# Score products on 64 rows in pairs, and a mask added by VectorE, in a one-core hybrid decoder layer

## The chip, the core and the metric

The kernel runs on one core of a Trainium2 chip. The core has TensorE (matrix products, PE in the rows; its weight loads are listed as PEld), VectorE (DVE), ScalarE (ACT), GpSimd (POOL) and SyncE (SP, which issues the DMAs). [...] The metric is the device time of one execution in microseconds; lower is better.

## What is computed

The reference is one decoder layer on 512 positions of width 1024: a token mixer (a gated MLP over chunks and a sparse attention), a cross-attention into 256 memory tokens, and a squared-ReLU MLP. The change touches the sparse attention. With 512 positions, top-16 selection picks all 8 blocks, so the selected branch and the window branch are both plain causal attention, each with keys and values of its own:

```python
s = jnp.einsum('bthgd,bhtmd->bhgtm', qc, kg) * scale
p = masked_softmax(s, mask)          # mask: key_pos <= t
o = g[..., 0:1] * o_cmp + g[..., 1:2] * o_slc + g[..., 2:3] * o_win
```

There are 8 query heads of 64 channels, in 2 groups of 4 that share a key head.

## The kernel before

**Precision.** Numbers that enter a product are split into a high part of type fp32r and a low part that is the rest. A product of two split operands is the sum of high x high, low x high and high x low, three TensorE products into one PSUM tile.

**Scores.** A query tile is 128 positions of one head. `qprep` puts the high and the low part of the query, 64 channels each, into one tile of 128 rows, `qT`. `KB` (its tile is called `b` in the trace) holds the high part of the keys on both halves of the rows, so that one product over 128 rows gives high x high plus low x high. `KL` holds the low part of the keys, on the half of the rows where the query's high part lies, and zeros on the other half, so that a second product over 128 rows gives high x low. A third product, `idb` (the identity) by `tri` (0 or -1e38, bf16), adds the causal mask to the last 128 columns. So a score tile is KB, KL, tri.

**Units and steps.** `units` lists (query tile t, key head, pair of heads): 4 x 2 x 2 = 16 units, and each unit takes two steps. Query tile t sees nb = t+1 key blocks, n = 128 nb columns a branch. For t = 0 and 1 ("early") both branches of a head fit in one bank (2n is 256 or 512 columns); for t = 2 and 3 ("late") each branch of a head has a bank of its own (384 or 512 columns). Before, step e of a unit does head e, both branches. `Pair.scores` makes the products, `Pair.soft` takes the row maximum on VectorE (TENSOR_REDUCE) and the exponential with its row sum on ScalarE, `Pair.scale` multiplies by gate over row sum, `Pair.turn` (one step pair later) transposes the probabilities on TensorE, and `Pair.values` multiplies them with the values.

**Order.** The program is recorded by a class `Plan` and issued in an order that its list scheduler works out: each engine has a fixed order when the program is built. The scheduler takes the costs of `Plan.cost` and a priority of each operation, its place in the program plus a number by stage out of the table `LEADS`. On TensorE, work of other stages (projections, output products) stands between the steps of the attention. The `w,b`, `w,q` and `b,w` products of the rows are such work.

Of the kernel before, what the change touches and what calls it, by code (L numbers as in the profile page):

```python
# [9 lines left out]
F32 = mybir.dt.float32  # L10
# [46 lines left out]
LEADS = {"ch_f0": -1174, "ch_f1": -1572, "ch_f2": -903, "ch_norm1": 1885, "ch_norm2": 867, "ch_norm3": -7928,  # L57
# [21 lines left out]


class Plan:
# [20 lines left out]
    def __init__(self, tc, share):  # L102
        self.tc, self.nc, self.share = tc, tc.nc, share
        self.ops, self.loads, self.lead, self.queue, self.stage, self.stages = [], [], 0.0, None, None, []
        self.home, self.last, self.reads, self.tables = {}, {}, {}, []
        self.tiles, self.uses, self.caps, self.index = [], [], {}, {}
        for e in self.ENGINES:
            setattr(self, e, self._Engine(self, e))
# [31 lines left out]
    def cost(self, eng, op, aps, func):  # L140
        n = max(self.width(a) for a, _ in aps)
        if eng == "tensor":
            if op == "transpose" and all(a.dtype == F32 for a, _ in aps):
                return 109
            return max(25, n / 2.4 + (15 if n > 200 else 7))
# [10 lines left out]
        if eng == "vector":  # L156
            if op == "reciprocal":
                return 68 + 6.3 * n
            fast = op in ("tensor_scalar", "tensor_copy") and not psum
            return 68 + n / (1.92 if fast else 0.96) + 61 * (scalars > (op == "tensor_reduce")) + part  # L160
# [43 lines left out]
    def add(self, ways, args, kw):  # L204
# [48 lines left out]
        func = next((a for a in args if isinstance(a, OP)), None)  # L253
        ways = [(self.ENGINES.index(e), op, self.cost(e, op, aps, func), self.locks(e, op, reads, writes))
                for e, op in ways]
        self.loads.append(self.load(ways[0][1], args[1]) if ways[0][0] == 0 else 0.0)
# [152 lines left out]
def hybrid_block(ctx, tc, x, mem, norm_mix_g, w_in, sg_ln_g, sg_ln_b, sg_w, sg_b, q_norm_g,  # L409
# [163 lines left out]
    load_x(0)  # L573
    dma(grw, norm_mix_g.rearrange("o (k p) -> (o k) p", p=P))
    w_inv = w_in.rearrange("o (k p) n -> p (o k) n", p=P)
# [90 lines left out]
    for h in range(NKV):  # L666
        pool.memset(KL[(1 - h) * HD:(2 - h) * HD, h].bitcast(F32), 0.0)
# [37 lines left out]
    def put_k(b, c):  # L705
# [26 lines left out]
        for h in range(NKV):  # L732
            nc.scalar.copy(KL[h * HD:h * HD + HD, h, b, :], low[h * HD:h * HD + HD, :])
# [35 lines left out]
    tri = cpool.tile([P, P], BF16, name="tri")  # L769
    tri32 = ztile()[:, :P]  # L770
    pool.memset(tri32, 0.0)
    pool.affine_select(out=tri32, in_=tri32, pattern=[[-1, P]], compare_op=OP.is_ge,
# [138 lines left out]
    def qprep(t, kvh):  # L911
# [6 lines left out]
        qs = qs.rearrange("p (g s d) -> p g s d", g=G, s=2)  # L918
        hi, lo = qs[:, :, kvh, :], qs[:, :, 1 - kvh, :]
# [3 lines left out]
        for g in range(G):  # L923
            nc.tensor.transpose(ps[:, g * P:g * P + P].bitcast(F32R), qs[:, g].rearrange("p s d -> p (s d)"), idr)
# [27 lines left out]
    class Pair:  # L952


        def __init__(self, t, kvh, pr, qT):
            self.t, self.kvh, self.pr, self.qT = t, kvh, pr, qT
            self.nb = t + 1
            self.n = self.nb * P
            self.blocks = [(b, j) for b in range(2) for j in range(self.nb)]
            self.S, self.Ps = [None] * 2, [None] * 2  # L960
            self.mx, self.den = [None] * 2, [None] * 2
            self.pts = None

        def scores(self, e):
            kvh, n = self.kvh, self.n
            g = 2 * self.pr + e
            q = self.qT[:, g * P:g * P + P]
            if 2 * n <= 512:
                S = bank()[:, :2 * n].rearrange("p (b n) -> p b n", b=2)
                for i, k in enumerate((KB, KL)):  # L970
                    nc.tensor.matmul(S, q, k[:, kvh, :, :n], start=i == 0, stop=False)
                nc.tensor.matmul(S[:, :, n - P:n], idb, bc(tri[:, None, :], [P, 2, P]), start=False, stop=True)
                self.S[e] = [S]
            else:
                self.S[e] = []
                for b in range(2):
                    S = bank()[:, :n]
                    for i, k in enumerate((KB, KL)):
                        nc.tensor.matmul(S, q, k[:, kvh, b, :n], start=i == 0, stop=False)
                    nc.tensor.matmul(S[:, n - P:n], idb, tri, start=False, stop=True)  # L980
                    self.S[e].append(S)
            self.mx[e], self.den[e] = small(2), small(2)
            self.Ps[e] = []

        def soft(self, e, b):
            Ss, mx = self.S[e], self.mx[e]
            if len(Ss) == 2:
                dve.tensor_reduce(mx[:, b:b + 1], Ss[b], AX.X, OP.max, negate=True)
            elif b == 0:
                dve.tensor_reduce(mx, Ss[0], AX.X, OP.max, negate=True)  # L990
            S = Ss[b] if len(Ss) == 2 else Ss[0][:, b, :]
            self.Ps[e].append(zpool.tile([P, 512], F32, tag="P", bufs=6, name=nm("P"))[:, :self.n])
            act(self.Ps[e][b], S, AF.Exp, bias=mx[:, b:b + 1], accum_out=self.den[e][:, b:b + 1])

        def scale(self, e):
            h = self.kvh * G + 2 * self.pr + e
            c = small(2)
            dve.reciprocal(c, self.den[e])
            for b in range(2):
                nc.either(("vector", "tensor_scalar"), ("gpsimd", "tensor_scalar"))(  # L1000
                    self.Ps[e][b], self.Ps[e][b], c[:, b:b + 1],
                                   gates[:, self.t, 3 * h + 1 + b:3 * h + 2 + b], OP.mult, OP.mult)

        def turn(self, e, q):

            if self.pts is None:
                self.pts = [b8([P, 2, 4, 2 * P], F32R) for _ in range((2 * self.nb + 3) // 4)]
            blk = self.blocks[4 * q:4 * q + 4]
            n = len(blk)
            if not n:  # L1010
                return None
            ps = bank()
            for i, (b, j) in enumerate(blk):
                nc.tensor.transpose(ps[:, i * P:i * P + P], self.Ps[e][b][:, j * P:j * P + P], idf)
            pv = ps[:, :n * P].rearrange("p (j t) -> p j t", j=n)
            pt = self.pts[q]
            return pv, pt[:, 0, :n, e * P:e * P + P], pt[:, 1, :n, e * P:e * P + P]

        def values(self, ptc):
            po = bank()[:, :2 * P]  # L1020
            for i, (b, j) in enumerate(self.blocks):
                if i == len(self.blocks) - 1:
                    for e in range(2):
                        for s in range(2):
                            nc.tensor.matmul(po[:, e * P:e * P + P], Vc[:, self.kvh, 2 * self.pr + e, :], ptc[:, s, :],
                                             start=False, stop=False)
                for s in range(2):
# [408 lines left out]
```

## Time and profile before

| what | value |
|---|---|
| median of 3 runs | 700.16 us (699.53 to 701.16) |
| profiled execution | 699.56 us, its span 697.8 us |
| PE busy | 689.5 us, 99% |
| DVE busy | 415.2 us, 59% |
| ACT busy | 318.2 us, 46% |
| granted TensorE clock | 1.00 all through |

The span runs from the first to the last instruction of the profiled execution; 1.76 us of its time lie around the span. A product's record is longer than the distance to the next one, since products overlap in the pipeline; what a product takes of TensorE's time is the distance between starts.

### The profile page before, as it was taken

How to read it: one execution, taken by the hardware profiler on the slowest of the kernel's cores; microseconds unless marked ns; L12 is line 12 of the kernel's file. 1: busy time of each engine (PE TensorE's matmuls, PEld its weight loads, DVE VectorE, ACT ScalarE, POOL GpSimd, SP SyncE). 2: the span in 40 equal slices, each digit the busy share in tenths (PEclk: the TensorE clock that was granted, in tenths of full speed). 3: DMA queues.
4: the chain of work that ended last, by engine and by line, in shares of the span. 5: the costliest groups of instructions: out<-in, count | busy, mean ns of one | idle time of the engine just before them, and what ended most of it. 6: DMA issues, size and time to landing. Idle time of an engine off the chain costs nothing.

```text
span 697.8 us, 9634 instructions
## 1 busy us (share of the span) xinstructions
PE 689.5 (99%) x3632; PEld 579.0 (83%) x3632; DVE 415.2 (59%) x791; ACT 318.2 (46%) x634; POOL 79.2 (11%) x120
## 2 busy tenths in 40 slices
PE   8999999999999999999999999999999999999997
PEld 7898878888888788888988888888878888888886
DVE  6578898898999997679842432223224444334423
ACT  6544558877788774586532341424133221112210
POOL 1101103232342130133000000000000000000000
PEclk9999999999999999999999999999999999999999
DMA  9624553552223101323243333323223222232203
GB/s 284 167 86 129 156 156 119 182 189 83 62 61 91 62 1 42 111 62 92 66 116 94 88 90 98 113 74 110 91 91 115 97 91 90 97 112 93 91 0 121
DMA packets 63677, 71.03 MB, mean 102 GB/s; under 512 B 3160, under 2 KB 46928, under 8 KB 63632
## 3 DMA queue, kind: packets, MB, share of 16 engines
q1 hardware_dynamic: 63632, 70.42, 32.8%
q8 instruction: 29, 0.48, 0.3%
q14 instruction: 16, 0.13, 0.1%
HBM read 68.32 MB, written 2.10 MB: 101 GB/s over the span
## 4 chain that ended last, share of the span: by engine, by line
PE 92%; DVE 3%; ACT 3%; DMA 1%; issue 0%; SPq 0%; DVEq 0%; ACTq 0%
PE ps L405 92%; DVE b L405 1%; DVE w L405 1%; ACT w L405 1%; ACT b L405 1%; DMA raw<-in_cmp_w_dram 1%; ACT P L405 1%; DMA raw<-in_w_in_dram 1%; DVE s L405 0%; ACT KL L405 0%; DVE pc L405 0%; ACT z L405 0%; DVE P L405 0%; SPq L405 0%; DVE q L405 0%
## 5 line engine op out<-in xcount | busy, mean ns | idle before, releaser
L405 PE MATMUL ps<-w,q 128*128 128x512 f32 x960 | 225.1, 391 | 0.7 <-ACT z L405 0.7
L405 ACT CAST w<-raw 128x1024 fp32r<-128x1024 f32 (+2 forms) x96 | 98.7, 1029 | 249.5 <-PE ps L405 239.9
L405 PEld LDWEIGHTS ps<-w,q 128*128 128x128 f32 x960 | 178.5, 188 | 37.2 <-ACT z L405 1.1
L405 DVE TENSOR_TENSOR w<-raw,w 128x1024 fp32r<-128x1024 f32 (+2 forms) x113 | 133.0, 1178 | 113.0 <-ACT w L405 112.4
L405 PE MATMUL ps<-w,b 128*128 128x512 f32 (+3 forms) x832 | 188.8, 377 | 0.9 <-DVE w L405 0.7
L405 PEld LDWEIGHTS ps<-w,b 128*128 128x128 f32 (+1 forms) x832 | 142.9, 186 | 27.4 <-DVE w L405 2.7
L405 PE MATMUL ps<-b,w 128*128 128x512 f32 x720 | 164.7, 389 | 0.0
L405 PEld LDWEIGHTS ps<-b,w 128*128 128x128 f32 x720 | 134.8, 188 | 27.9
L405 DVE TENSOR_TENSOR b<-ps,b 128x512 fp32r<-128x512 f32 (+2 forms) x88 | 54.6, 636 | 9.4 <-ACT b L405 6.4
L405 PE MATMUL ps<-b,b 128*128 128x256 f32 x344 | 58.7, 293 | 0.0
L405 DVE CAST q<-b 128x512 fp32r<-128x512 f32 x27 | 11.5, 427 | 70.6 <-PE ps L405 70.5
L405 ACT CAST b<-ps 128x512 fp32r<-128x512 f32 (+1 forms) x84 | 44.0, 552 | 17.6 <-PE ps L405 16.9
L405 PEld LDWEIGHTS ps<-b,b 128*128 128x128 f32 x344 | 49.1, 192 | 1.4
L405 POOL TENSOR_SCALAR P<-P,s,gates 128x128 f32<-128x128 f32 (+3 forms) x55 | 35.4, 653 | 90.2 <-DVE s L405 76.9
L405 ACT ACTIVATE P<-ps,s 128x128 f32<-128x128 f32 (+3 forms) x64 | 33.5, 532 | 4.5 <-DVE s L405 4.3
L405 PE MATMUL ps<-idf,P 128*128 128x128 f32 x192 | 34.9, 281 | 0.0
L405 DVE TENSOR_REDUCE s<-ps 128x2 f32<-128x512 f32 (+3 forms) x56 | 32.5, 602 | 0.3 <-PE ps L405 0.2
L405 POOL TENSOR_TENSOR r<-s,negh 128x1 f32<-128x1 f32 (+2 forms) x25 | 20.2, 808 | 93.9 <-DVE s L405 93.8
L405 ACT ACTIVATE z<-ps 128x512 f32<-128x512 f32 (+3 forms) x43 | 23.0, 581 | 11.6 <-PE ps L405 11.5
L405 DVE TENSOR_TENSOR q<-b,q 128x512 fp32r<-128x512 f32 (+1 forms) x36 | 23.7, 657 | 4.6 <-ACT q L405 3.7
L405 PE MATMUL ps<-b,q 128*128 128x256 f32 (+2 forms) x96 | 26.0, 339 | 0.2 <-ACT q L405 0.2
L405 PEld LDWEIGHTS ps<-idf,P 128*128 128x128 f32 x192 | 23.5, 141 | 1.3
(154 smaller groups left out, 549.3 us busy)
## 6 DMA issues: line engine op xcount, KB each, us to landing
raw<-in_w_ff_dram SPq DMA_DIRECT2D x64, 512.0 KB, 4.0
raw<-in_w_in_dram SPq DMA_DIRECT2D x12, 512.0 KB, 4.5
raw<-in_cmp_w_dram SPq DMA_DIRECT2D x8, 512.0 KB, 4.3
raw<-in_w_out_dram SPq DMA_DIRECT2D x8, 512.0 KB, 3.8
raw<-in_w_mkv_dram SPq DMA_DIRECT2D x8, 512.0 KB, 3.8
b<-in_x_dram SPq DMA_DIRECT2D x8, 256.0 KB, 5.1
raw<-in_w_in_dram SPq DMA_DIRECT2D x8, 256.0 KB, 5.6
b<-in_x_dram SPq DMA_DIRECT2D x4, 512.0 KB, 5.7
```

The costliest lines, as they stand in the source:

```text
L405: getattr(getattr(self.nc, eng), op)(*a, **k)
```

## The change

It does four things. The KL products of the two heads of a unit are done on 64 rows each, head 0 on rows 0 to 63 and head 1 on rows 64 to 127, one after the other in the program; for this `qprep` lays out the second head with low and high swapped, and KL holds the low keys on both halves (four more copies on ScalarE, no zeroing on GpSimd). A late step now does one branch of both heads in place of both branches of one head (`part`). Late score tiles get no tri product: VectorE adds the mask, takes the negated sum's minimum and writes the scores to SBUF in one instruction (`tensor_tensor_reduce`, in the rows ISA with a second, small ISA on `s`), and the exponential reads SBUF. Early tiles keep the tri product. The scheduler's cost of the first product of a pair is 4, and `LEADS` has new numbers throughout.

```diff
@@ Plan.cost, Plan.add
+            if self.beside:
+                self.beside = False
+                return 4
...
+        next_to = self.ops and self.ops[-1][0][0][2] == 4
...
@@ LEADS
-LEADS = {"ch_f0": -1174, "ch_f1": -1572, "ch_f2": -903, "ch_norm1": 1885, "ch_norm2": 867, "ch_norm3": -7928,
+LEADS = {"ch_f0": 528, "ch_f1": -1424, "ch_norm0": -3838, "ch_norm1": -9550, "ch_norm3": -11668,
...
@@ put_k
-            nc.scalar.copy(KL[h * HD:h * HD + HD, h, b, :], low[h * HD:h * HD + HD, :])
+            for half in (0, HD):
+                nc.scalar.copy(KL[half:half + HD, h, b, :], low[h * HD:h * HD + HD, :])
@@ Pair.scores
-                for i, k in enumerate((KB, KL)):
-                    nc.tensor.matmul(S, q, k[:, kvh, :, :n], start=i == 0, stop=False)
-                nc.tensor.matmul(S[:, :, n - P:n], idb, bc(tri[:, None, :], [P, 2, P]), start=False, stop=True)
...
+                for e in heads:
+                    nc.tensor.matmul(S[e], q[e], KB[:, kvh, b, :n], start=True, stop=False)
+
+                for e in heads:
+                    r = slice(e * HD, e * HD + HD)
+                    nc.beside = e == 0
+                    nc.tensor.matmul(S[e], q[e][r], KL[r, kvh, b, :n], start=False, stop=not self.both)
+                for e in heads:
+                    if self.both:
+                        nc.tensor.matmul(S[e][:, :, n - P:n], idb, bc(tri[:, None, T - P:], [P, 2, P]),
+                                         start=False, stop=True)
@@ Pair.soft, late tiles
-                dve.tensor_reduce(mx[:, b:b + 1], Ss[b], AX.X, OP.max, negate=True)
...
+                dve.tensor_tensor_reduce(out=pt, in0=S, in1=tri[:, T - self.n:], scale=-1.0, scalar=3e38,
+                                         op0=OP.add, op1=OP.min, accum_out=mx[:, i:i + 1])
+                act(pt, pt, AF.Exp, bias=mx[:, i:i + 1], scale=-1.0, accum_out=self.den[x][:, i:i + 1])
```

The order on TensorE, at the first late unit (t = 2, key head 0). Names in a row are out<-moving,stationary; `ps_452` and `ps_453` are two score tiles, `b_9_89` is KB, `q_449` the query tile. Before:

```order
L405 MATMUL ps_452<-b_9_89,q_449 128x384
L405 MATMUL ps_452<-KL,q_449 128x384
L405 LDWEIGHTS idb
L405 MATMUL ps_452<-tri,idb 128x128
L405 MATMUL ps_453<-b_9_89,q_449 128x384
L405 MATMUL ps_453<-KL,q_449 128x384
L405 LDWEIGHTS idb
L405 MATMUL ps_453<-tri,idb 128x128
```

The same place of the changed kernel, with the row before and behind:

```order
L411 MATMUL ps_766<-w_765,b_640_735 128x512 x2
L411 MATMUL ps_452<-b_9_89,q_449 128x384
L411 MATMUL ps_453<-b_9_89,q_449 128x384
L411 MATMUL ps_452<-KL,q_449 128x384
L411 MATMUL ps_453<-KL,q_449 128x384
L411 MATMUL ps_457<-idf,P_439 128x128 x2
```

The two KL products (64 rows each now) stand next to each other, the tri products are gone, and products over 128 rows stand on both sides.

A later late step on TensorE (t = 2, key head 1; `ps_519` and `ps_520` are the score tiles, `ps_517` a tile of `values`). Before:

```order
L405 MATMUL ps_519<-b_9_89,q_504 128x384
L405 MATMUL ps_519<-KL,q_504 128x384
L405 LDWEIGHTS idb
L405 MATMUL ps_519<-tri,idb 128x128
L405 MATMUL ps_514<-idf,P_487 128x128
L405 MATMUL ps_517<-b_388_482,b_10_91 128x256 x5
L405 MATMUL ps_520<-b_9_89,q_504 128x384
L405 MATMUL ps_520<-KL,q_504 128x384
```

The changed kernel there:

```order
L411 MATMUL ps_519<-b_9_89,q_504 128x384
L411 MATMUL ps_519<-KL,q_504 128x384
L411 MATMUL ps_514<-idf,P_487 128x128
L411 MATMUL ps_517<-b_388_482,b_10_91 128x256 x2
L411 MATMUL ps_517<-b_389_483,b_10_91 128x256 x4
L411 MATMUL ps_517<-pt_476,Vc 128x128
L411 MATMUL ps_514<-idf,P_487 128x128
L411 MATMUL ps_520<-b_9_89,q_504 128x384
L411 MATMUL ps_520<-KL,q_504 128x384
L411 MATMUL ps_517<-pt_476,Vc 128x128 x3
```

Here the two KL products of the pair don't stand together: products over 128 rows lie between them. Of the 24 pairs in the changed order 18 stand together (all 8 early ones, 5 late ones of 384 columns and 5 of 512) and 6 stand apart (3 of 384, 3 of 512). An early pair is followed by its two tri products:

```order
L411 MATMUL ps_280<-b_9_89,q_278 128x256
L411 MATMUL ps_281<-b_9_89,q_278 128x256
L411 MATMUL ps_280<-KL,q_278 128x256
L411 MATMUL ps_281<-KL,q_278 128x256
L411 LDWEIGHTS idb
L411 MATMUL ps_280<-tri,idb 128x256
L411 LDWEIGHTS idb
L411 MATMUL ps_281<-tri,idb 128x256
```

In this piece the tri products have moved from behind each head's KL product to behind both.

## Rows read from the trace of the kernel before

**Rows 1.** The page: span, busy time of TensorE, TensorE in 40 slices, its clock.
```profile
span 697.8 us, 9634 instructions
PE 689.5 (99%) x3632; PEld 579.0 (83%) x3632; DVE 415.2 (59%) x791; ACT 318.2 (46%) x634; POOL 79.2 (11%) x120
...
PE   8999999999999999999999999999999999999997
...
PEclk9999999999999999999999999999999999999999
```

**Rows 2.** Windows: early steps, t = 2, t = 3; busy us (count) of each engine.
```profile
97.00:179.80 82.80, 82.41 (x483) 68.98 (x481) 73.94 (x184) 64.67 (x164) 22.44 (x38) 1.00 0.43 135
179.80:219.00 39.20, 39.20 (x261) 33.24 (x260) 36.19 (x96) 31.94 (x83) 12.06 (x16) 1.00 0.28 86
219.00:258.00 39.00, 38.84 (x259) 31.68 (x258) 36.94 (x88) 30.08 (x75) 11.45 (x15) 1.00 0.11 36
```

**Rows 3.** Groups of TensorE by shape: rows*columns, out, count, busy us, mean ns.
```profile
L405 PE MATMUL ps<-b,w 128*128 128x512 f32 x720 | 164.7, 389 | 0.0
...
L405 PE MATMUL ps<-tri,idb 128*128 128x128 bf16 x32 | 7.4, 230 | 0.0
...
L405 PE MATMUL ps<-q,z 128*64 128x64 f32 x12 | 0.8, 220 | 0.0
```

**Rows 4.** Timeline of TensorE at a late step: start us, length us, what.
```profile
200.87 0.34 PE L405 MATMUL ps<-b,q 128*128 128x384 f32 x1
201.04 0.34 PE L405 MATMUL ps<-KL,q 128*128 128x384 f32 x1
201.22 0.23 PE L405 MATMUL ps<-tri,idb 128*128 128x128 bf16 x1
201.26 0.42 PE L405 MATMUL ps<-b,q 128*128 128x384 f32 x1
201.52 0.34 PE L405 MATMUL ps<-KL,q 128*128 128x384 f32 x1
...
201.76 0.28 PE L405 MATMUL ps<-idf,P 128*128 128x128 f32 x1
201.88 0.27 PE L405 MATMUL ps<-idf,bT 128*128 128x128 f32 x1
```

**Rows 5.** Timeline of TensorE around two 64-row transposes, 108.9 to 111.2 us.
```profile
108.93 0.84 PE L405 MATMUL ps<-w,b 128*128 128x512 f32 x3
109.70 0.25 PE L405 MATMUL ps<-idr,z 64*128 64x64 f32 x1
109.88 0.33 PE L405 MATMUL ps<-idf,wg 128*128 128x128 f32 x1
109.96 0.48 PE L405 MATMUL ps<-w,b 128*128 128x512 f32 x1
110.37 0.24 PE L405 MATMUL ps<-idr,z 64*128 64x64 f32 x1
110.54 0.97 PE L405 MATMUL ps<-w,b 128*128 128x512 f32 x3
```

**Rows 6.** The weight loads of the same stretch.
```profile
109.16 0.19 PEld L405 LDWEIGHTS ps<-w,b 128*128 128x128 f32 x1
109.70 0.14 PEld L405 LDWEIGHTS ps<-idr,z 64*128 64x128 f32 x1 [0.35 <-issue]
...
110.36 0.14 PEld L405 LDWEIGHTS ps<-idr,z 64*128 64x128 f32 x1 [0.24 <-issue]
```

**Rows 7.** Groups of VectorE by shape.
```profile
L405 DVE TENSOR_TENSOR b<-ps,b 128x512 fp32r<-128x512 f32 x64 | 43.0, 685 | 7.2 <-ACT b L405 6.4
...
L405 DVE TENSOR_REDUCE s<-ps 128x1 f32<-128x512 f32 x16 | 10.4, 676 | 0.0
...
L405 DVE TENSOR_SCALAR s<-s 128x1 f32<-128x1 f32 x22 | 3.3, 148 | 2.3 <-ACT j L405 1.3 <-ACT z L405 1.0
```

**Rows 8.** The group of ScalarE that writes KL.
```profile
L405 ACT CAST KL<-ps 64x512 fp32r<-64x512 f32 x4 | 2.3, 583 | 0.0
```

More of the change, by code (lines that the diff above doesn't have):

```diff
@@ L144, in cost @@
                 return 109
+            if self.beside:
+                self.beside = False
+                return 4
             return max(25, n / 2.4 + (15 if n > 200 else 7))
@@ L159, in cost @@
             fast = op in ("tensor_scalar", "tensor_copy") and not psum
+            if op == "tensor_tensor_reduce":
+                part += 60
             return 68 + n / (1.92 if fast else 0.96) + 61 * (scalars > (op == "tensor_reduce")) + part
@@ L253, in add @@
         func = next((a for a in args if isinstance(a, OP)), None)
+        next_to = self.ops and self.ops[-1][0][0][2] == 4
         ways = [(self.ENGINES.index(e), op, self.cost(e, op, aps, func), self.locks(e, op, reads, writes))
                 for e, op in ways]
-        self.loads.append(self.load(ways[0][1], args[1]) if ways[0][0] == 0 else 0.0)
+        self.loads.append(self.load(ways[0][1], args[1]) if ways[0][0] == 0 and not next_to else 0.0)
         self.tables.append(next((self.TABLES[a] for a in args if isinstance(a, AF) and a in self.TABLES), None))
@@ L573, in hybrid_block @@
     load_x(0)
+    nc.stage = "gain0"
     dma(grw, norm_mix_g.rearrange("o (k p) -> (o k) p", p=P))
+    nc.stage = "kv"
     w_inv = w_in.rearrange("o (k p) n -> p (o k) n", p=P)
@@ L665, in hybrid_block @@
     KL = cpool.tile([P, NKV, 2, T], F32R, name="KL")
-    for h in range(NKV):
-        pool.memset(KL[(1 - h) * HD:(2 - h) * HD, h].bitcast(F32), 0.0)
     VB = b8([P, 2 * NKV * TT, P], F32R)
@@ L768, in hybrid_block @@
     dve.tensor_copy(idb, idf)
-    tri = cpool.tile([P, P], BF16, name="tri")
-    tri32 = ztile()[:, :P]
+    tri = cpool.tile([P, T], BF16, name="tri")
+    tri32 = ztile()
     pool.memset(tri32, 0.0)
-    pool.affine_select(out=tri32, in_=tri32, pattern=[[-1, P]], compare_op=OP.is_ge,
+    pool.affine_select(out=tri32[:, T - P:], in_=tri32[:, T - P:], pattern=[[-1, P]], compare_op=OP.is_ge,
                        fill=NEG, base=0, channel_multiplier=1)
@@ L917, in qprep @@
         qs, qT = qpair()
-        qs = qs.rearrange("p (g s d) -> p g s d", g=G, s=2)
-        hi, lo = qs[:, :, kvh, :], qs[:, :, 1 - kvh, :]
+        hi = bass.AP(qs.tensor, qs.offset, [list(qs.ap[0]), [4 * HD, 2], [3 * HD, 2], [1, HD]])
+        lo = bass.AP(qs.tensor, qs.offset + HD, [list(qs.ap[0]), [4 * HD, 2], [HD, 2], [1, HD]])
+        qv = qv.rearrange("p (a e) d -> p a e d", e=2)
         nc.either(("scalar", "copy"), ("vector", "tensor_copy"))(hi, qv)
@@ L923, in qprep @@
         for g in range(G):
-            nc.tensor.transpose(ps[:, g * P:g * P + P].bitcast(F32R), qs[:, g].rearrange("p s d -> p (s d)"), idr)
+            nc.tensor.transpose(ps[:, g * P:g * P + P].bitcast(F32R), qs[:, g * P:g * P + P], idr)
         nc.scalar.copy(qT, ps)
@@ L958, in __init__ @@
             self.n = self.nb * P
+            self.both = 2 * self.n <= 512
             self.blocks = [(b, j) for b in range(2) for j in range(self.nb)]
-            self.S, self.Ps = [None] * 2, [None] * 2
+            self.S, self.Ps = {}, {}
             self.mx, self.den = [None] * 2, [None] * 2
             self.pts = None
-        def scores(self, e):
-            kvh, n = self.kvh, self.n
[L966 to L969, printed above, removed]
-                for i, k in enumerate((KB, KL)):
-                    nc.tensor.matmul(S, q, k[:, kvh, :, :n], start=i == 0, stop=False)
-                nc.tensor.matmul(S[:, :, n - P:n], idb, bc(tri[:, None, :], [P, 2, P]), start=False, stop=True)
-                self.S[e] = [S]
-            else:
[L975 to L983, printed above, removed]
@@ L985, in soft @@
-        def soft(self, e, b):
-            Ss, mx = self.S[e], self.mx[e]
-            if len(Ss) == 2:
-                dve.tensor_reduce(mx[:, b:b + 1], Ss[b], AX.X, OP.max, negate=True)
[L989 to L993, printed above, removed]
@@ L995, in scale, with slot, part, scores @@
-        def scale(self, e):
-            h = self.kvh * G + 2 * self.pr + e
+        def slot(self, b, j):
+            return b * (self.nb if self.both else 4) + j
+        def part(self, x, i):
+            return (x, i) if self.both else (i, x)
+        def scores(self, x):
+            kvh, n = self.kvh, self.n
+            if x == 0 or not self.both:
+                b = slice(0, 2) if self.both else slice(x, x + 1)
+                heads = range(2)
+                q = [self.qT[:, (2 * self.pr + e) * P:(2 * self.pr + e + 1) * P] for e in heads]
+                S = [bank()[:, :n * (b.stop - b.start)].rearrange("p (b n) -> p b n", n=n) for e in heads]
+                for e in heads:
[8 more added lines that the diff above has]
+                                         start=False, stop=True)
+                    for i in range(b.start, b.stop):
+                        self.S[e, i] = S[e][:, i - b.start, :]
+                    if self.both:
+                        self.S[e] = S[e]
+            self.mx[x], self.den[x] = small(2), small(2)
@@ new lines, in soft @@
+        def soft(self, x, i):
+            e, b = self.part(x, i)
+            mx, S = self.mx[x], self.S[e, b]
+            self.Ps[e, b] = pt = zpool.tile([P, 512], F32, tag="P", bufs=6, name=nm("P"))[:, :self.n]
+            if self.both:
+                if i == 0:
+                    dve.tensor_reduce(mx, self.S[e], AX.X, OP.max, negate=True)
+                act(pt, S, AF.Exp, bias=mx[:, i:i + 1], accum_out=self.den[x][:, i:i + 1])
+            else:
+                dve.tensor_tensor_reduce(out=pt, in0=S, in1=tri[:, T - self.n:], scale=-1.0, scalar=3e38,
+                                         op0=OP.add, op1=OP.min, accum_out=mx[:, i:i + 1])
+                act(pt, pt, AF.Exp, bias=mx[:, i:i + 1], scale=-1.0, accum_out=self.den[x][:, i:i + 1])
@@ L997, in scale @@
+        def scale(self, x):
             c = small(2)
-            dve.reciprocal(c, self.den[e])
-            for b in range(2):
+            dve.reciprocal(c, self.den[x])
+            for i in range(2):
+                e, b = self.part(x, i)
+                h = self.kvh * G + 2 * self.pr + e
                 nc.either(("vector", "tensor_scalar"), ("gpsimd", "tensor_scalar"))(
-                    self.Ps[e][b], self.Ps[e][b], c[:, b:b + 1],
-                                   gates[:, self.t, 3 * h + 1 + b:3 * h + 2 + b], OP.mult, OP.mult)
@@ L1004, in turn @@
-        def turn(self, e, q):
+                    self.Ps[e, b], self.Ps[e, b], c[:, i:i + 1],
+                    gates[:, self.t, 3 * h + 1 + b:3 * h + 2 + b], OP.mult, OP.mult)
+        def turn(self, x):
             if self.pts is None:
[L1007 to L1017, printed above, removed]
+                self.pts = [b8([P, 2, 4, 2 * P], F32R) for _ in range(1 if self.both else 2)]
+            parts = [[(x, b, j) for b, j in self.blocks]] if self.both else [
+                [(e, x, j) for j in range(self.nb)] for e in range(2)]
+            r = []
+            for part in parts:
+                n = len(part)
+                ps = bank()
+                for i, (e, b, j) in enumerate(part):
+                    nc.tensor.transpose(ps[:, i * P:i * P + P], self.Ps[e, b][:, j * P:j * P + P], idf)
+                pt = self.pts[0 if self.both else x]
+                r.append((ps[:, :n * P].rearrange("p (j t) -> p j t", j=n), pt[:, 0, :n, e * P:e * P + P],
+                          pt[:, 1, :n, e * P:e * P + P]))
+            return r
@@ L1026, in values @@
                                              start=False, stop=False)
+                k = self.slot(b, j)
                 for s in range(2):
-                    nc.tensor.matmul(po, VBv[:, b, self.kvh, j, :], self.pts[i // 4][:, s, i % 4, :],
+                    nc.tensor.matmul(po, VBv[:, b, self.kvh, j, :], self.pts[k // 4][:, s, k % 4, :],
                                      start=i == 0 and s == 0, stop=i == len(self.blocks) - 1 and s == 1)
@@ L1065, in hybrid_block @@
         old = pairs.get(jt) if 0 <= jt < len(units) else None
-        sp = [old.turn(e, q) if old else None for q in range(2)]
+        sp = old.turn(e) if old else []
         for i in range(2):
@@ L1074, in hybrid_block @@
             nc.stage = f"turn{k}"
-            if sp[i]:
+            if i < len(sp):
                 nc.scalar.copy(sp[i][1], sp[i][0])
         for q in sp:
-            if q:
-                dve.tensor_tensor(q[2], q[0], q[1].bitcast(F32), OP.subtract)
+            dve.tensor_tensor(q[2], q[0], q[1].bitcast(F32), OP.subtract)
         nc.stage = f"val{k}"
```

40 rows, old and new, of the table LEADS are left out of this document.

## The prediction

> **What bounds the kernel now.** [...] Then the windows of the attention [rows 2]: in the late stages TensorE is busy 39.20 of 39.20 us (t = 2) and 38.84 of 39.00 us (t = 3). VectorE is close behind there, 36.19 and 36.94 us, so 3.0 + 2.1 = 5.1 us idle over both; ScalarE has 16 us of room. Then the groups for the price of a slot, and the timeline for what happens at a border between kinds of product, which the groups hide, because records overlap.
>
> A slot is the distance between starts in an unbroken stream. 720 products of 512 columns take 164.7 us [rows 3], 0.229 us each. A 384-column one is 201.04 - 200.87 = 0.17 to 201.22 - 201.04 = 0.18 us [rows 4]; I use 0.175. For 256 columns, which only early tiles use, I take half of 0.229, 0.115.
>
> **Term 1: the late tri products go.** There are 32 of 128 columns [rows 3]. From the first KL product at 201.04 to the next KL product at 201.52 are 0.48 us [rows 4]; without the mask it would be two slots, 0.35, so the mask costs 0.13 us: 0.04 until the next start, and the rest because the next product waits for its weights. The second, before a transpose, costs 201.76 - 201.52 - 0.175 = 0.065 us. Both kinds of neighbour occur; I take 0.10, so 32 x 0.10 = 3.2 us are saved (bounds 2.1 and 4.2).
>
> **Term 2: the KL products on 64 rows.** If two such products run side by side, a pair takes one slot in place of two. Nowhere in the trace do two 64-row products on different rows follow each other, so whether they overlap is bounded by nothing (two slots as before) and by all (one slot saved). The pairs that stand together are 4 of 256, 4 + 5 of 512 and 5 of 384 columns: one slot each is 4 x 0.115 + 9 x 0.229 + 5 x 0.175 = 3.4 us. I take the overlap as full, since the pair uses different rows and different banks.
>
> But the trace does show what a 64-row instruction between 128-row ones costs [rows 5]. The third of the three products at 108.93 starts near 109.38 (0.84 less the last record's 0.39 behind 108.93). The 64-row transpose starts at 109.70, 0.32 us later in place of 0.23. [...] Over the whole stretch, from 109.38 to the last start of the final group (110.54 + 0.97 - 0.39 = 111.12), 1.74 us pass. The work in it is four 512-column slots (0.92), one 128-wide transpose (201.88 - 201.76 = 0.12 [rows 4]) and two 64-column products at 0.8/12 = 0.07 us [rows 3]; that is 1.17. So two visits to 64 rows cost 0.57 us beyond their own work, 0.29 each. A KL product's weights take longer to load than a transpose's (records of 0.19 and 0.14 us [rows 6]), and on both borders the load now lies bare: I take 0.35 a visit, bounds 0.30 and 0.40.
>
> [...]
>
> Now count visits in the new order. Late pairs that stand together are one visit each: five of 512 columns lose 0.35 - 0.229 = 0.12, five of 384 lose 0.35 - 0.175 = 0.175, together 1.5 us lost. The six pairs that stand apart are twelve visits, with no overlap to be had: 12 x 0.35 = 4.2 us lost. At the eight early pairs the mask follows, whose neighbours wait for their weights in either kernel; I leave 0.10 of a visit out: 4 x (0.25 - 0.115) + 4 x (0.25 - 0.229) = 0.6 us lost. Term 2 is a loss of 6.3 us.
>
> **Term 3: VectorE's mask.** The new instruction reads PSUM and SBUF and writes SBUF like the 685 ns TENSOR_TENSOR, and replaces a reduce of 676 ns [rows 7]. It comes with a small second one; the nearest small VectorE row is 148 ns. So 0.16 us more for each of 32, 5.0 us, against the 5.1 us that VectorE is idle in these stages plus the 2.5 us by which TensorE's late stage gets longer (1.5 + 4.2 - 3.2). Behind it on VectorE are the low halves of transposed probabilities, which `values` waits for; as long as it fits into the idle time, other TensorE work stands between. I take nothing. Bounds: nothing, and an instruction that takes two passes (685 + 676 ns).
>
> **Term 4: the rest.** Four more KL copies on ScalarE of 583 ns [rows 8]: two more in each of two stages, before any score product; covered by the projections that TensorE does then. If that cover is gone, it is 2 x 0.58 = 1.2 us. The exponential from SBUF and the copies of 3 + 3 in place of 4 + 2 blocks are off the bound. The new numbers in LEADS can't take more than the idle TensorE time, 697.8 - 689.5 = 8.3 us, much of which is start and end, unchanged in the first DMAs; I take nothing.
>
> **Sum.** -3.2 + 6.3 = +3.1 us on the profiled execution's 699.56, 702.7. The median of the runs shown, 700.16, is 0.6 above that execution, so I predict 703.3 us.
>
> **Rivals.**
> *No price at the border* (the other side). If the wait in the 64-row rows belongs to transposes or to the tiny products, and 64-row score products stream in like others, the change saves 3.2 + 3.4 = 6.6 us: 693.6 us. For it: all 64-row rows here are transposes. Against it: the 128-row transposes at 201.76 and 201.88 follow the instruction ahead by 0.06 and 0.12 us [rows 4], so being a transpose costs no such pause. It decides from a visit of 0.25 us: the net loss of 3.1 us over 30 visits (18 pairs and 12 single products) is 0.10 each, so at 0.35 - 0.10 the kernel stays as it is, and below that it is faster. [...]
> *The border costs and the pair doesn't overlap.* Then the 3.4 us are lost as well: 703.3 + 3.4 = 706.7 us. For it: no overlap is seen anywhere in the trace; against it: nothing in the rows that ties the two halves.
> *VectorE becomes the bound in the late stages.* With two passes the 32 instructions add about 20 us (16 x 0.685, 16 x 0.55) and 4.7 for the small ones, against 7.6 of room: some 17 us, 720 us. It decides from 7.6 / 32 = 0.24 us extra for each. For it: VectorE is 94% busy there already.
> *The order gains.* The new LEADS take 2 to 3 us of stalls away: 700.5 to 701.
>
> **Chances.** Forecast 0.56, its own range 700.5 to 706.5 (0.05 a visit either way is 1.5 us, the mask 1.0, the copies 1.2). No price 0.20; no overlap 0.14; VectorE 0.04; order 0.06. To leave no more than 2 in 10 out, the range must reach into the no-price case below: 693 to 708. A difference under 0.2%, 1.4 us, is about what can't be told from none here. Faster takes the no-price case and the edge of the others, 0.24; the same 0.16; slower 0.60.
>
> **What would show it.** Each KL group as 64*128, and in the timeline its first weight load starting some 0.1 us late with "issue" before it. In a pair that stands together, two KL starts within 0.11 us of each other and the next 128-row load about 0.3 us behind for 512 columns (overlap), or about 0.5 us (none). No tri rows after 180 us, and KB starts 0.175 apart there. TensorE busy near 99% still: if its idle time grows by more than 2 us with VectorE as releaser in the late windows, term 3 is wrong. If KL's loads run ahead as others do, term 2 is wrong and the time is near 693.6.

## The result, and the profile after

| what | changed kernel | before, beside it |
|---|---|---|
| median | 705.25 us (704.72 to 706.02, 4 runs) | 700.6 us (699.53 to 701.16, 4 runs) |
| ratio | 1.0069 [1.0052, 1.0086] | 1 |
| profiled execution | 705.22 us, span 703.5 us | 699.56 us, span 697.8 us |

The kernel got slower by 0.69%, 4.65 us by the medians. The forecast was 703.3 us, 3.1 us above the median of 700.16 that it started from; the time lies inside its own range (700.5 to 706.5).

The page of the changed kernel, as [rows 1] of before:

```profile
span 703.5 us, 9589 instructions
PE 695.4 (99%) x3600; PEld 578.0 (82%) x3600; DVE 424.2 (60%) x834; ACT 307.0 (44%) x626; POOL 74.3 (11%) x119
...
PE   9999999999999999999999999999999999999997
...
PEclk9999999999999999999999999999999999999999
```

TensorE has 32 instructions fewer and is busy 5.9 us longer. Its idle time is what it was (703.5 - 695.4 = 8.1 us against 8.3), and the clock is the same. So as a whole the loss isn't idle time of TensorE; its stream takes longer.

The windows of the same three stages, with boundaries between the same steps (columns as in [rows 2]):

```profile
97.00:182.50 85.50, 84.76 (x491) 69.42 (x490) 74.19 (x183) 62.92 (x162) 21.84 (x38) 1.00 0.41 135
182.50:223.00 40.50, 40.50 (x242) 32.61 (x241) 35.13 (x102) 31.18 (x80) 9.28 (x15) 1.00 0.25 79
223.00:265.00 42.00, 41.04 (x238) 30.67 (x237) 37.40 (x108) 29.60 (x74) 11.92 (x16) 1.00 0.08 26
```

VectorE is now idle for 5.4 + 4.6 us in the late stages, more than the 5.1 us of [rows 2], although it has taken over the mask. The mask instruction is listed as CUSTOM_DVE_ANT_0 and its small second part as DVE_READ_ACCUMULATOR2_ANT (groups of VectorE, as [rows 7]):

```profile
L411 DVE CUSTOM_DVE_ANT_0 P<-ps,tri 128x512 f32<-128x512 f32 x16 | 10.6, 684 | 0.9 <-PE ps L411 0.8
...
L411 DVE CUSTOM_DVE_ANT_0 P<-ps,tri 128x384 f32<-128x384 f32 x16 | 8.4, 549 | 0.2
...
L411 DVE DVE_READ_ACCUMULATOR2_ANT s<- 128x1 f32 x32 | 2.6, 82 | 0.0
```

One pass of 684 ns replaces a reduce of 676 ns [rows 7], and the small second part is 82 ns: 0.09 us more for each of the 32, 2.9 us in all, inside the idle time.

Now TensorE at the first late pair, by the timeline (start us, length us, what):

```profile
183.75 0.64 PE L411 MATMUL ps<-w,b 128*128 128x512 f32 x2
184.23 0.52 PE L411 MATMUL ps<-b,q 128*128 128x384 f32 x2
184.68 0.44 PE L411 MATMUL ps<-KL,q 64*128 64x384 f32 x2
185.05 0.66 PE L411 MATMUL ps<-idf,P 128*128 128x128 f32 x4
```

Both KL products together last 0.44 us, and the transposes behind them start 0.37 us after the pair does. A KL product that stands alone lasts as long:

```profile
196.49 0.22 PE L411 MATMUL ps<-pt,Vc 128*128 128x128 f32 x1
196.64 0.44 PE L411 MATMUL ps<-KL,q 64*128 64x384 f32 x1
197.00 0.55 PE L411 MATMUL ps<-pt,Vc 128*128 128x128 f32 x3
```

So the second product of a pair adds nothing that the timeline shows: the records of the two start 3 or 4 ns apart in each of the 18 pairs that stand together.

But one product, or one pair, holds TensorE for 0.36 to 0.37 us, where a slot of 384 columns over 128 rows is 0.175 us. The weight loads around the single product:

```profile
196.37 0.19 PEld L411 LDWEIGHTS ps<-pt,Vc 128*128 128x128 f32 x1
196.64 0.18 PEld L411 LDWEIGHTS ps<-KL,q 64*128 64x128 f32 x1
197.00 0.41 PEld L411 LDWEIGHTS ps<-pt,Vc 128*128 128x128 f32 x3 [0.18 <-issue]
```

Neither load runs ahead here. KL's starts with its own product at 196.64, and the next 128-row load starts at 197.00, after the load path stood still for 0.18 us. The view of tile KL counts these pauses (engine op x count: length in ns, least, median, most):

```profile
L411 PEld LDWEIGHTS ps<-KL,q x48: 182/183/184, 101.6 to 264.0; 64*128 64x128 f32 x48
L411 PE MATMUL ps<-KL,q x48: 379/466/502, 101.6 to 264.0; 64*128 64x512 f32 x24, 64*128 64x384 f32 x16, 64*128 64x256 f32 x8
...
  issue: 7.0, 24
```

It has 24 idle pauses ahead of KL that nothing but "issue" ends, 7.0 us in all: the sign that the prediction named, but at 0.29 us each it is longer than the 0.1 us put down there. So is the other distance that it named: behind a pair of 512 columns the next product comes 0.43 us later, in place of 0.3, although the pair overlaps.

```profile
238.25 0.49 PE L411 MATMUL ps<-KL,q 64*128 64x512 f32 x2
238.68 0.33 PE L411 MATMUL ps<-idf,P 128*128 128x128 f32 x1
```

### The profile page after: what moved, and what is told of

It is laid out like the page before. It is cut to its first block, busy times and chain, and to the rows that moved or that the text cites. A ratio compares the mean times of both kernels' runs of the same rounds, so it can differ in the third digit from the quotient of the medians.

```text
span 703.5 us, 9589 instructions
## 1 busy us (share of the span) xinstructions
PE 695.4 (99%) x3600; PEld 578.0 (82%) x3600; DVE 424.2 (60%) x834; ACT 307.0 (44%) x626; POOL 74.3 (11%) x119
## 4 chain that ended last, share of the span: by engine, by line
PE 94%; DVE 3%; ACT 1%; DMA 1%; issue 0%; DVEq 0%; ACTq 0%
PE ps L411 94%; DVE b L411 1%; DMA raw<-in_cmp_w_dram 1%; DVE w L411 1%; ACT b L411 1%; ACT w L411 0%; DVE s L411 0%; ACT P L411 0%; DVE pc L411 0%; DVE bT L411 0%; ACT z L411 0%; DVE P L411 0%; DVEq L1461 0%; DVE z L411 0%; DVE zero L411 0%
## 5 line engine op out<-in xcount | busy, mean ns | idle before, releaser
L411 PE MATMUL ps<-w,b 128*128 128x512 f32 (+2 forms) x832 | 187.8, 376 | 1.1 <-DVE w L411 0.6
L411 ACT CAST w<-raw 128x1024 fp32r<-128x1024 f32 (+1 forms) x73 | 74.4, 1019 | 175.4 <-PE ps L411 162.1
L411 DVE CAST w<-raw 128x1024 fp32r<-128x1024 f32 (+2 forms) x40 | 26.8, 671 | 75.5 <-PE ps L411 72.2
L411 DVE TENSOR_TENSOR b<-ps,b 128x512 fp32r<-128x512 f32 (+3 forms) x88 | 54.3, 636 | 8.7 <-ACT b L411 6.5
L411 ACT CAST b<-ps 128x512 fp32r<-128x512 f32 (+2 forms) x84 | 44.4, 553 | 19.9 <-PE ps L411 19.1
L411 PE MATMUL ps<-b,q 128*128 128x256 f32 (+2 forms) x96 | 22.5, 331 | 0.2 <-ACT q L411 0.2
L411 PE MATMUL ps<-idf,z 128*128 128x128 f32 (+1 forms) x108 | 21.6, 279 | 0.3 <-DVE s L411 0.3
## 6 DMA issues: line engine op xcount, KB each, us to landing
b<-in_x_dram SPq DMA_DIRECT2D x8, 256.0 KB, 5.8
raw<-in_w_in_dram SPq DMA_DIRECT2D x8, 256.0 KB, 5.8
```

What stands on the lines that cost most here:

```text
L411: getattr(getattr(self.nc, eng), op)(*a, **k)
```

## The experiments

Ten kernels were run, each beside the kernel before on the same chip. Most ratios of 1% and less come from 12 runs. Single executions differ by up to 1.6 us in the first 12 us, where TensorE's wait for the first data (`b<-in_x_dram`) is 1.5 us in one trace and not listed in another, so traces are compared by stages and medians for the whole. Two kinds of edit must be told apart in what follows. Some edits leave the scheduler's order of every engine as it is (an instruction is swapped or left out when it is issued); others let the scheduler work it out anew. The expectations name runs by short labels: e1 is the first experiment here, e6 the mask alone with its order kept, and e8 the run that takes the early masks from e6.

### KL over 128 rows again, in the changed order

```diff
-nc.tensor.matmul(S[e], q[e][r], KL[r, kvh, b, :n], start=False, stop=not self.both)
+nc.tensor.matmul(S[e], q[e], KL[:, kvh, b, :n], start=False, stop=not self.both)
```

KL gets its zeros back, and `qprep` its old layout. The order of TensorE stays.

> The changed kernel with its KL products over 128 rows again (zeros on the other half of KL, query tiles laid out as before), everything else and TensorE's order kept to the row. Theory A (each stay on 64 rows costs 0.35 to 0.39 us and the pair overlaps fully): 30 stays are gone and 18 slots come back, so 705.25 - 6.3 to - 7.4, about 698 to 699 us. Theory B (no price at the border; the loss is the new order's stalls and VectorE): only the overlap goes, 705.25 + 3.4 = 708.6 us.

Measured: 699.55 us, 0.9977 [0.9964, 0.9990]. The 64 rows cost 0.92% (1.0069 against 0.9977, 6.5 us; 5.7 by the two medians), and without them the change is a small gain: this version beats both kernels. The same place of its trace:

```profile
184.31 0.64 PE L411 MATMUL ps<-w,b 128*128 128x512 f32 x2
184.79 0.52 PE L411 MATMUL ps<-b,q 128*128 128x384 f32 x2
185.15 0.51 PE L411 MATMUL ps<-KL,q 128*128 128x384 f32 x2
185.50 0.60 PE L411 MATMUL ps<-idf,P 128*128 128x128 f32 x4
```

From the first KB to the transposes are 0.71 us here and 0.82 in the changed kernel (185.05 - 184.23): two slots of 0.175 beat one overlapped pair with its borders. Since TensorE's order is the same, each stay on 64 rows can be priced so. I took the time from the instruction ahead of it to the second behind it, in the changed kernel less in this one:

| kind of stay | count | mean extra us, measured | predicted |
|---|---|---|---|
| late pair, 384 columns | 5 | 0.18 | 0.175 |
| late pair, 512 columns | 5 | 0.10 | 0.12 |
| late single product | 12 | 0.37 | 0.35 |
| early pair, 256 columns | 4 | 0.17 | 0.135 |
| early pair, 512 columns | 4 | 0.07 | 0.02 |

These add up to 0.9 + 0.5 + 4.4 + 0.7 + 0.3 = 6.8 us; the prediction had 6.3. (One early pair of 512 columns is followed by transposes and not by its tri products, and cost 0.12 us; the other three cost 0.05.)

### Both heads' KL on the same 64 rows

```diff
-r = slice(e * HD, e * HD + HD)
+r = slice(kvh * HD, kvh * HD + HD)
```

`qprep` has its old layout here too, so that the high half of both heads lies on these rows, and KL holds the low keys there alone. The order and the number of stays are those of the changed kernel.

> The changed kernel with both heads' KL products on the same 64 rows, so that they can't run side by side; same order, same number of stays. Theory A (overlap is full): 18 slots come back, 705.25 + 3.4 = 708.7 us, and the second KL start of a pair is a slot behind the first in place of 3 ns. If the overlap were worth nothing: 705.25 us.

Measured: 709.0 us, 1.0113 [1.0093, 1.0133], 3.75 us above the changed kernel. The pair of the timeline above:

```profile
186.14 0.52 PE L411 MATMUL ps<-b,q 128*128 128x384 f32 x2
186.59 0.62 PE L411 MATMUL ps<-KL,q 64*128 64x384 f32 x2
187.13 0.66 PE L411 MATMUL ps<-idf,P 128*128 128x128 f32 x4
```

The transposes come 0.54 us after the pair's start in place of 0.37: one slot of 384 columns more. The second KL product starts 0.28 us behind the first, not one slot of 0.175 as was expected, and the transposes 0.27 us behind it; the sum is what it should be. So the overlap is real and full, and the 3.75 us are near what was put down for it (3.4). It also shows that a further product on the same 64 rows adds 0.17 us, about its slot; the first, with the way to 64 rows and back, takes the other 0.37.

### 64 rows in the kernel before, each product alone

```diff
-nc.tensor.matmul(S, q, k[:, kvh, b, :n], start=i == 0, stop=False)
+nc.tensor.matmul(S, q, KB[:, kvh, b, :n], start=True, stop=False)
+r = slice(kvh * HD, kvh * HD + HD)
+nc.tensor.matmul(S, q[r], KL[r, kvh, b, :n], start=False, stop=False)
```

> The kernel before, order kept to the row on TensorE, with each KL product over only the 64 rows that hold numbers. No two stand together, so this is 48 stays on 64 rows and no overlap. Theory A (0.37 us a stay, 0.1 less at the 16 early ones, whose mask product waits for its weights anyway): 48 x 0.37 - 1.6 = +16.2, about 717 us. Theory B (no price at the border): 700.6 us.

Measured: 713.39 us, 1.0180 [1.0157, 1.0204]; 12.5 us for 48 stays, 0.26 each. The rival without a border price, 700.6, is out, in an order where nothing else of the change is present. The size was missed by 3.7 us. Here a mask product follows nearly every stay, and its neighbours wait for their weights in either kernel (ahead of the load of `idb` the load path stands still for 0.16 us in the kernel before and for 0.18 us here); I had allowed for that at the early tiles only. By the starts of the same instructions a stay with the mask product directly behind it costs 0.28 us, at early and late tiles alike; three that have a product of another kind there cost 0.34 to 0.39. A late step of this run (start us, length us, what):

```profile
186.12 0.33 PE L405 MATMUL ps<-b,q 128*128 128x384 f32 x1
186.38 0.44 PE L405 MATMUL ps<-KL,q 64*128 64x384 f32 x1
186.75 0.23 PE L405 MATMUL ps<-tri,idb 128*128 128x128 bf16 x1
186.79 0.42 PE L405 MATMUL ps<-b,q 128*128 128x384 f32 x1
187.14 0.44 PE L405 MATMUL ps<-KL,q 64*128 64x384 f32 x1
```

From one KL product to the next are 0.76 us against 0.48 in [rows 4]: 0.28 a stay.

### All pairs together

A dependence and a high priority keep each pair's second product behind its first; the scheduler orders the rest anew.

```diff
+nc.also, nc.lead = [len(nc.ops) - 1], nc.lead + 1e5
 for e in heads:
     nc.tensor.matmul(S[e], q[e][r], KL[r, kvh, b, :n], ...)
+nc.also, nc.lead = [], nc.lead - 1e5
```

> The changed kernel with all 24 pairs standing together: the first KL product of a pair is made to wait for both KB products in the scheduler, and both get a high priority. Theory A: six stays and six slots fewer, 6 x (0.37 + 0.20) = 3.4 us, 701.8 us. Theory B: six slots fewer, 1.2 us, 704.0 us. The order elsewhere shifts a little, 1 us either way.

Measured: 711.5 us, 1.0155 [1.0130, 1.0180], a miss by 10 us. All 24 pairs stand together here, but the order around them changed too. TensorE's waits come to 8.8 us, 5.0 more than in the changed kernel, and the largest is new (releaser: us in total, times, longest):

```profile
PE ps L412 <- DVE z L412: 3.9, 2, 3.3
```

The wait of 3.3 us ends at 258.9 us, and from 257.9 to 264.7 us the granted clock is 0.50 (columns as in [rows 2]):

```profile
257.90:264.70 6.80, 5.43 (x20) 4.07 (x21) 5.41 (x17) 2.17 (x6) 0.00 (x0) 0.50 0.01 2
```

The instructions of this stretch take some 2.7 us longer than the same kinds elsewhere in this run and in the changed kernel (an estimate from the distances between starts). The span is 5.1 us longer than the changed kernel's (708.6 against 703.5). With 5.0 us of waits and 2.7 us of lower clock in it, 2.6 us are left as a gain of the pairs and of the order around them together, where 3.4 were expected; the run doesn't separate these two.

### The mask alone, order worked out anew

The kernel before with the late mask by `tensor_tensor_reduce`, its LEADS unchanged.

```diff
-nc.tensor.matmul(S[:, n - P:n], idb, tri, start=False, stop=True)
...
-dve.tensor_reduce(mx[:, b:b + 1], Ss[b], AX.X, OP.max, negate=True)
+dve.tensor_tensor_reduce(out=pt, in0=Ss[b], in1=tri[:, T - self.n:], ..., accum_out=mx[:, b:b + 1])
```

> The kernel before with one part of the change: late tiles masked by VectorE with the maximum, no late tri products; KL over 128 rows, heads and steps and the priority table as before. Theory A: 700.6 - 3.2 = 697.4 us. Theory B (VectorE's longer instruction costs what TensorE gains): 700.6 us or more.

Measured: 727.29 us, 1.0365 [1.0336, 1.0393], a miss by 30 us. TensorE's waits come to 20.8 us; the largest:

```profile
PE ps L407 <- DVE pc L407: 5.3, 1, 5.3
PE ps L407 <- DVE b L407: 3.7, 2, 3.4
PE ps L407 <- POOL P L407: 2.4, 6, 1.0
```

Twice the granted clock is at 0.50 or 0.51 for 3.4 us, once from 1.6 us after the end of the wait of 3.4 us on (it ends at 212.7), and once from 0.7 us before the end of the wait of 5.3 us on (it ends at 256.0):

```profile
214.30:217.70 3.40, 3.39 (x13) 3.30 (x14) 2.31 (x9) 1.53 (x5) 0.00 (x0) 0.51 0.01 2
255.30:258.70 3.40, 2.73 (x10) 2.33 (x11) 2.07 (x6) 0.29 (x2) 0.00 (x0) 0.50 0.00 0
```

### The mask alone, order kept

The same idea, with every engine's order held: each late tri product is left out where it stood, and each reduce is replaced where it stood (in place in PSUM).

```diff
+nc.swap[len(nc.ops) - 1] = lambda m: None                 # the late tri product
...
+nc.swap[len(nc.ops) - 1] = lambda m, ...: m.vector.tensor_tensor_reduce(
+    out=S, in0=S, in1=triw[:, T - self.n:], ..., accum_out=x)   # the reduce
```

> The kernel before with its order kept, in which the 32 late tri products are left out and the late maximum is the changed kernel's VectorE instruction, here writing the masked scores back to PSUM so that no buffer moves. Theory A (a tri product costs TensorE 0.10 us, VectorE's extra 0.09 us lies in its idle time): 700.6 - 3.2 = 697.4 us. Theory B (VectorE is what got worse in the run with the mask alone, 727 us, and not the order): well over 701 us.

Measured: 700.7 us, 0.9997 [0.9981, 1.0013]. So the mask's work on VectorE is not what cost the run before it 26.6 us: its waits on TensorE are 16 us longer than the 4.7 us of this run, and two stretches of lower clock go with them. That leaves the scheduler's new order. (The two runs also differ in where the masked scores go, to SBUF there and to PSUM here; the first experiment writes them to SBUF and is fast.) But the 3.2 us of term 1 don't appear either. In place the accumulator read is slower, 139 ns against 82 (by groups of VectorE):

```profile
L1002 DVE DVE_READ_ACCUMULATOR2_ANT s<- 128x1 f32 x32 | 4.4, 139 | 0.0
```

Two readings were left: VectorE is late with its longer work, or TensorE's saved time isn't to be had in this order.

### No late mask at all, order kept

The same without VectorE's part: the late tri products are left out and the plain reduce stays.

> The kernel before, order kept, with the 32 late tri products left out and nothing in their place: late tiles are not masked, VectorE's maximum is as before. It asks why e6 gained nothing (0.9997). Theory V (VectorE's extra 5 us of e6, 32 x (0.02 + 0.14), filled its 5.1 us of idle time in the late stage, and TensorE waited for it): without them the 3.2 us come out, 697.5 us. Theory W (in the old order TensorE's late stage waits for VectorE anyway, even without extra work): 700 us or more.

Measured: 700.15 us, 0.9995 [0.9980, 1.0010]: no gain that can be told, with no work added anywhere. The place in the trace where TensorE now waits (idle us and releaser in brackets):

```profile
195.53 0.42 PE L408 MATMUL ps<-b,q 128*128 128x384 f32 x1
195.79 0.34 PE L408 MATMUL ps<-KL,q 128*128 128x384 f32 x1
196.33 0.52 PE L408 MATMUL ps<-idf,P 128*128 128x128 f32 x3 [0.20 <-ACT P L408]
```

Before, a tri product stood at this gap, and the transposes followed it at once:

```profile
196.66 0.33 PE L405 MATMUL ps<-KL,q 128*128 128x384 f32 x1
196.84 0.23 PE L405 MATMUL ps<-tri,idb 128*128 128x128 bf16 x1
196.90 0.50 PE L405 MATMUL ps<-idf,P 128*128 128x128 f32 x3
```

Now they wait for ScalarE's exponential, and that has waited for VectorE's maximum:

```profile
195.52 0.58 ACT L408 ACTIVATE P<-ps,s 128x384 f32<-128x384 f32 x1 [1.27 <-DVE s L408]
```

In the kernel before this exponential starts at 195.83, so it comes 0.31 us earlier, while TensorE had gained 0.87 us by then. On VectorE the maximum stands behind a split of weights of 1.22 us, in both runs. By the starts of the same instructions the profiled execution gains 1.0 us of the expected 3.2 between 180 and 261 us: 3.3 us come out at the places of the tri products, and 2.3 us are given back in such holes, some of them too short for the list of waits. VectorE's instructions end 0.1 us earlier at 180 us and 1.1 us earlier at 260, no more than TensorE keeps.

### The late tri products back, in the changed order

The version of the first experiment, with 32 tri products issued behind the late KL products; VectorE's mask stays, so the late mask is added twice.

```diff
+nc.then[len(nc.ops) - 1] = lambda m, ...: m.tensor.matmul(o, idb, tri[:, T - P:], start=False, stop=True)
```

> The kernel of e1 (changed order, KL over 128 rows) with the 32 late tri products put back on TensorE behind each late KL product; VectorE adds its mask as well. TensorE then does all the work of the kernel before, in the new order. If a tri product costs 0.10 us: 699.55 + 3.2 = 702.8 us, and the new order by itself is worth +2 us against the kernel before. If the new order is as good as the old: 700.6 us, and a tri product costs 0.03 us.

Measured: 702.12 us, 1.0016 [1.0003, 1.0029], 2.6 us above the first experiment. So in the new order the tri products are worth 0.08 us each by the medians, with about 1 us of doubt on the 2.6. By the starts of the same instructions 3.3 us come out between 178 and 262 us, 0.10 each: 3.7 us at the places where they stood, of which only 0.4 are given back. And this kernel does all that TensorE did before, in the new order: 1.2 us more than the kernel before (between 0.2 and 2.0 by the interval). VectorE's mask and the late steps by branch are in it too, so the 1.2 us are not LEADS alone. Its waits of TensorE between 92 and 270 us:

```profile
PE ps L414 <- DVE s L414: 0.6, 2, 0.3
PE ps L414 <- DVE pc L414: 0.4, 1, 0.4
PE ps L414 <- POOL P L414: 0.4, 1, 0.4
```

With the three smaller rows (0.3, 0.2, 0.2) they are 2.1 us; in the kernel before, the same stretch has 0.6.

### Early masks by VectorE too

Two runs take the early tri products away as well, with the order kept: one on the mask-alone kernel whose order was kept, one on the version of the first experiment. VectorE gets two mask instructions for each early maximum instead.

```diff
+nc.swap[len(nc.ops) - 1] = lambda m: None                 # the early tri product
```

> e6 with the early tri products replaced as well: each early maximum over two branches becomes two of VectorE's masking instructions. Order kept. TensorE saves 16 x 0.13 = 2.1 us more; VectorE pays 16 x 0.3 = 5 us more in a stage where it is idle 8.9 us. 695.3 us if that is hidden; if it is not, TensorE waits behind it and the time is 697 to 700 us.

> e1 (changed order, KL over 128 rows, late masks by VectorE) with the 16 early tri products replaced too, two masking VectorE instructions for each early maximum, order kept. TensorE's stream gets 16 x 0.13 = 2.1 us shorter, VectorE pays 5 us in a stage in which it is idle 11 us. If VectorE's idle time can be used: 697.4 us. If TensorE waits behind VectorE as in e8, which gained nothing from the same step in the old order: 699.5 us.

Measured: 701.02 us, 1.0000 [0.9987, 1.0012], and 700.12 us, 0.9994 [0.9983, 1.0005]. Neither gains on the run that it started from (700.7 and 699.55). So in the new order, too, TensorE's time doesn't come out here; whether VectorE's added work takes it, these runs don't separate. In the second, the largest wait of TensorE is for VectorE's `pc`, with 1.1 us:

```profile
PE ps L414 <- DVE pc L414: 1.1, 2, 0.7
```

## Why the prediction was right, and where its sizes were off

The runs divide the change into three parts: the new order with all of TensorE's old work, +1.2 us (702.12 against 700.87); the late tri products out, -2.6 (699.55 against 702.12); KL on 64 rows, +5.7 (705.25 against 699.55). The sum is +4.3, and +4.65 was measured beside the change itself. Each part has about 1 us of doubt; by the ratios they are +1.1, -2.7 and +6.5. The prediction had 0, -3.2 and +6.3, +3.1 in all: its two large terms were near, the errors in them cancel by the medians, and most of the 1.5 us that it fell short is the first part, which it had put at nothing.

**What bounds the kernel**: the forecast counts what is added to TensorE's stream, or taken from it, as time of the kernel, since TensorE is busy for 99% of the span [rows 1]. That held for additions: each late stay on 64 rows went straight into the time (5.9 us by the starts, term 2). For removals it held only for the late tri products in the new order, and not in the old one. That is the finding the prediction hadn't seen: a TensorE that is busy 39.20 of 39.20 us [rows 2] is not yet TensorE alone on the bound. In the old order the chain through VectorE and ScalarE arrives just in time, so two thirds of the work taken out leave holes (2.3 of 3.3 us in the run with no late mask).

**Term 1** (-3.2): measured -2.6 by the medians and -3.3 by the starts, in the order in which it was done, inside the bounds of 2.1 and 4.2. In the old order it would have been nothing that can be told by the medians, 1.0 us by the starts.

**Term 2** (+6.3): the loss is shown from both sides, by taking the 64 rows out of the changed kernel and by putting them alone into the kernel before. By single stays it is 6.8 us, by medians 5.7 (6.5 by the ratios). By the starts of the same instructions between 97 and 265 us it is 6.6: 0.7 in the early stage and 5.9 in the late ones. The price read off two transposes of 64 columns [rows 5, 6] carried over to products of 384 and 512 columns, 0.37 against 0.35. Those rows give 0.29 of the 0.35; what was put on for a load that lies bare on both borders was an estimate that no run shows by itself. What the runs show is the whole stay: in the changed kernel KL's load takes 0.18 us and starts with its own product, and a single product costs 0.37 us more than over 128 rows. That the overlap would be full was an estimate too; it is shown by the starts, 3 or 4 ns apart on different rows and 0.28 us on the same rows. The largest share are the twelve products whose pairs the order tears apart, 4.4 us: they pay the borders without any overlap. With all pairs together the kernel would by these prices be some 3.6 us better (12 x 0.37 less 3 x 0.18 and 3 x 0.10), an estimate of 701.6 us, and still no gain over KL on 128 rows, since five pairs of each width, at 0.18 and 0.10 us, lose as well. The run meant for it doesn't settle this, because it changed the order; what is left of it behind its waits and its lower clock, 2.6 us, is of that size.

**Term 3** (nothing): right. The mask is 0.09 us more an instruction, not 0.16, and the point of 0.24 from which VectorE would decide was never near.

**Term 4** (nothing) is the step that was mis-sized. The new order, with VectorE's mask in it, costs 1.2 us, with 1.5 us more of waits between 92 and 270 us (2.1 against 0.6), for results of VectorE, GpSimd and ScalarE. I had put it at nothing because I had looked at LEADS only as a possible gain, bounded by TensorE's idle time.

**The rivals.** No price at the border would be near 699.55 or below: out by 6 us. No overlap would be 709.0 by the run made for it: out. VectorE as the bound: out by its idle time, 10.0 us in the late windows. A gain by the order: out, it costs 1.2 us. The traces show a pause of TensorE on both borders between 64 and 128 rows: KL's load starts with its own product, behind up to 0.36 us in which the load path does nothing (the pair at 238.25 us of the changed kernel), the next 128-row load starts 0.18 us after KL's has ended (196.64) and 0.24 us after it (238.25), and a single product pays 0.28 to 0.37 us for entering and leaving. Which step in the engine the pause is spent on, no run here shows.

## What to carry to other kernels

Before a product is put on half the rows, price the stay: here a pair that stood together still lost 0.18 us at 384 columns and 0.10 us at 512, so that entering and leaving cost more than the overlapped slot saved. That it could pay where several such pairs stand in a row is an estimate from these prices, which no run here has tried. Test one part of a change with every engine's order held: the same mask read 727 us with a re-derived order and 700.7 with the order kept. And TensorE's busy share of 99% told here that added work goes into the time, but not what removed work gives: in the old order 2.3 of the 3.3 us taken out were given back, so look first whether the engines that it waits for are early.

## What the hardware showed unexpectedly

A pair of 64-row products of fp32r lasts as long as one of them, 0.44 us at 384 columns, to the 0.01 us of the timeline, each with its own score tile and its own weights. And the vector instruction that adds, takes the minimum and writes out is one pass of 684 ns for 512 columns (the reduce that it replaces: 676), whose small second part took 82 ns when the large output went to SBUF and 139 ns when it went back to PSUM. And in the two re-ordered runs with waits of 3.3 us and more on TensorE the granted clock was at 0.50 or 0.51 for 3.4 to 6.8 us around or just after them; what set it, no run here shows. The mean granted clock of their profiled executions is 0.995, and that of all others 0.999 or 1.0.
